# The last projection of a decoder layer, token-major: the residual is turned to tokens by VectorE and the output is stored by tokens

## The chip, the cores and the metric

The kernel runs on one core of a Trainium2 chip. The metric is the time of one execution in microseconds on the device. The kernel before was timed three times: 2201.19, 2201.46 and 2201.54 us, so its median is 2201.46 us.

## The reference, cut to what matters

The program is one decoder layer for 256 tokens of width 2048: a half SwiGLU block (hidden width 5632), a token-mixing block (sparse attention beside an mLSTM), and a second half SwiGLU block. Only the very end is touched here:

```python
def rms_norm(x, gain):
    y = x32 * lax.rsqrt(jnp.mean(x32 * x32, axis=-1, keepdims=True) + EPS)
    return y * gain

def swiglu(x, w_gate, w_up, w_down):
    return (jax.nn.silu(x @ w_gate) * (x @ w_up)) @ w_down

x = x + 0.5 * swiglu(rms_norm(x, ffn2_norm), ffn2_w_gate, ffn2_w_up, ffn2_w_down)
return x                                  # (1, 256, 2048), float32
```

The last projection is the product of the hidden values, 256 tokens by 5632, with `ffn2_w_down`, 5632 by 2048. The factor 1/rms of a token is taken out of the norm: the hidden values lack it once more, so that the last product is multiplied by 0.5 and by that token's factor before it is added to the residual.

## The kernel before, in words

**Numbers.** All weights are float32 in HBM. A weight tile (`raw`, 128 x 1024, 512 KB) comes in through the SyncE queue. ScalarE rounds it to fp32r (`whi`, an instruction that the profile calls CAST), VectorE subtracts and rounds the rest (`wlo`). Activations are kept in the same two halves, high and low. A product is the sum of three: high by high, high by low and low by high. A 128 x 1024 weight tile thus gives TensorE the same 6144 columns of moving data in every projection, cut in one of two ways.

**Token-major units** (`unit_b`, the gate and up projections). The stationary operand is a 128 x 128 piece of the activations (`XX`), the moving operand is 512 columns of the weights. The result has tokens on the partitions. A weight tile holds 2 blocks of 128 rows by 512 columns. For each block and each of the two halves of the tokens stand three matmuls of 512 columns: 12 in a tile.

**Channel-major units** (`unit_a`, the down projections and some of the mixing block). The stationary operand is a 128 x 128 piece of the weights, the moving operand is the activations of all 256 tokens. The result has channels on the partitions. A weight tile holds 4 blocks of 128 rows by 256 columns. The high and the low half of the activations lie side by side, so one matmul of 512 columns takes `whi` by both, and one of 256 columns takes `wlo` by the high half: 16 matmuls in a tile, 8 of each width. The upper and lower half of the result of the former, 256 columns each, have to be added afterwards (`fold`: a ScalarE copy and a VectorE add).

**The last projection before.** The hidden values H are channel-major (44 blocks of 128 channels, high and low). Seven channel-major units of 256 output channels and 11 weight tiles each are followed by a residual step: fold, times 0.5 and the token's factor (`RB`, the factors spread over all partitions), add to X (channel-major, in SBUF), store 128 x 2 x 256. The eighth unit (`unit_last`) has three matmuls of 256 columns for each block and each of two groups of 128 channels, 24 in a tile, and its last weight tile takes all of the first group before all of the second. So `store_last` can multiply, add and store the first group while TensorE does the second. Both groups lie in one PSUM tile. The output is 2048 channels by 256 tokens and is transposed on the host, which is no part of the time.

**What sets the order.** The program is written as one list of units; each weight tile is worked on in two halves. After each half the main loop lets at most one waiting job take a step, and issues the split of the tile that is three ahead (`whi` after the first half, `wlo` after the second). Four buffers each hold `raw`, `whi` and `wlo`. A job is a chain of pieces, each yielding between its instructions; an estimate of the engines' times decides whether one may step (`step`), and `force` runs a job to its end at once. A job may not step while both PSUM side banks (the tags "sc" or "tr") are held. Engines execute in the order in which this loop issues; each instruction waits on semaphores for its inputs and buffers.

**Turning.** `turn` moves a 128 x 512 token-major block of hidden values to channels with VectorE transposes of 32 x 32 pieces: an instruction takes 32 partitions by 256 elements, and 16 make a block of 4 x 128 channels by 256 tokens. `g_turn` is the job that does it, four instructions at a time. The last such block of the second FFN is turned during the first tiles of the down projection.

Of the kernel before, what the change touches and what calls it, by code (L numbers as in the profile page):

```python
# [9 lines left out]
F32 = mybir.dt.float32  # L10
# [4 lines left out]
OP = mybir.AluOpType  # L15
# [3 lines left out]
S = 256  # L19
D = 2048  # L20
FF = 5632
EPS = 1e-6
NEG = -1e30
KD = D // 128
KF = FF // 128
# [89 lines left out]
def layer(ctx: ExitStack, tc: tile.TileContext, xt, cols, w_small, b_in,  # L115
          wg1, wu1, wd1, w_in, cw1k, cw2k, cw1v, cw2v, wb_n, wb_m, w_out, wg2, wu2, wd2, out):
    nc = tc.nc
    est = Estimate()
    V, A, T, G = (Engine(e, n, est) for e, n in ((nc.vector, "V"), (nc.scalar, "A"), (nc.tensor, "T"), (nc.gpsimd, "G")))
# [10 lines left out]
    def nm(p):  # L130
        uid[0] += 1
        return f"{p}{uid[0]}"
# [18 lines left out]
    X = per.tile([128, KD, S], F32, name="X")  # L151
# [10 lines left out]
    RB = per.tile([128, S], F32, name="RB")  # L162
# [4 lines left out]
    def col(i, n=1):  # L167
        return cl[:, i:i + n]
# [14 lines left out]
    cur = {}  # L183
# [7 lines left out]
    def job(gen, name=None, need=(), rank=0):  # L191
        jobs.append([est.end, gen, name, need, rank])
        jobs.sort(key=lambda j: j[4])
# [55 lines left out]
    def mul(*a, **k):  # L249

        T.matmul(*a, **k)
        for _ in range(min(len(small_ones), 2 + len(small_ones) % 2)):
            small_ones.popleft()()
# [9 lines left out]
    def force(name):  # L263
        settle()
        while name not in past:
            j = next(j for j in jobs if j[2] == name)
            for n in j[3]:
                force(n)
            if step(j):
                uptake(j)  # L270
# [64 lines left out]
    def blocks(w, c0, ncol, kts):  # L335

        nk = 1024 // ncol
        v = w.rearrange("(k p) n -> p k n", p=128)
        return [(v[:, k:k + nk, c0:c0 + ncol], nk, ncol) for k in range(0, kts, nk)]
# [29 lines left out]
    def unit_last(w, c0, ncol, kts, act, done):  # L369

        nk = 1024 // ncol

        def emit(ps, h, e, wh, wl):
            a = act()
            end = h == kts // nk - 1
            for k in range(nk) if end else range(e * nk // 2, (e + 1) * nk // 2):
                kt = nk * h + k
                for c in (e,) if end else range(2):
                    cs = slice(c * 128, c * 128 + 128)
                    mul(ps[:, c, 0:S], wh[:, k, cs], a[:, kt, 0, :], start=kt == 0, stop=False)  # L380
                    mul(ps[:, c, 0:S], wh[:, k, cs], a[:, kt, 1, :], start=False, stop=False)
                    mul(ps[:, c, 0:S], wl[:, k, cs], a[:, kt, 0, :], start=False, stop=kt == kts - 1)
        u = Unit(blocks(w, c0, ncol, kts), emit, lambda ps: done(ps, 1))
        u.mid = lambda ps: done(ps, 0)
        return u
# [4 lines left out]
    def fold(o, ps, c=2):  # L390

        A.copy(o, ps[:, 0:c, S:])
        V.tensor_add(o, ps[:, 0:c, 0:S], o)

    units = []
# [23 lines left out]
    def residual(pool, c, ps, half, gcol, name):  # L419

        y = pool.tile([128, 2, S], F32, name=nm("y"), tag="y", bufs=2)
        fold(y, ps)
        if half:
            V.scalar_tensor_tensor(y, y, 0.5, rb2(), op0=OP.mult, op1=OP.mult)
        xc = X[:, 2 * c:2 * c + 2, :]
        V.tensor_add(xc, xc, y)
        if gcol is None:
            nc.sync.dma_start(ov[:, 2 * c:2 * c + 2, :], xc)
            return
        for kt in (2 * c, 2 * c + 1):  # L430
            A.activation(XH[:, kt, :], X[:, kt, :], AF.Identity, scale=col(gcol + kt))
            V.scalar_tensor_tensor(XL[:, kt, :], X[:, kt, :], col(gcol + kt), XH[:, kt, :].bitcast(F32),
                                   op0=OP.mult, op1=OP.subtract)
        if c == 0:
            A.activation(acc, xc, AF.Square)
            return
        sq = pool.tile([128, 2, S], F32, name=nm("sq"), tag="y", bufs=2)
        A.activation(sq, xc, AF.Square)
        V.tensor_add(acc, acc, sq)
        if c == 7:  # L440
            job(g_r(), name)

    ov = out.rearrange("(k p) t -> p k t", p=128)

    def store_last(pool, ps, k):
        y = pool.tile([128, S], F32, name=nm("y"), tag="y", bufs=2)
        kt = KD - 2 + k
        V.scalar_tensor_tensor(y, ps[:, k, 0:S], 0.5, RB, op0=OP.mult, op1=OP.mult)
        V.tensor_add(X[:, kt, :], X[:, kt, :], y)
        nc.sync.dma_start(ov[:, kt, :], X[:, kt, :])  # L450

    def rb2():
        return RB[:, None, :].to_broadcast([128, 2, S])

    def turn(o, h, j):

        ov_ = o.rearrange("p k (t q f) -> p t k q f", t=2, f=32)
        hv = h.rearrange("p t (k q f) -> p t k q f", q=4, f=32)
        for i in range(4):
            V.transpose(ov_[32 * j:32 * j + 32, :, :, i, :], hv[32 * i:32 * i + 32, :, :, j, :])  # L460


    def ffn(wg, wu, wd, first, nxt, name):


        env = {}

        def open_pool():
            p = tc.tile_pool(name=nm("ffn"), bufs=1)
            env["pool"] = p  # L470
            env["p"] = cur["ffn"] = p.__enter__()
            env["H"] = env["p"].tile([128, KF, 2, S], F32R, name=nm("H"), tag="h")

        def close_pool():
            env["pool"].__exit__(None, None, None)

        def gate_done(c):
            def f(ps):
                if c == 1:
                    force(first + "up")  # L480
                if c:
                    force(name + "h%d" % (c - 1))
                g = env["g", c] = env["p"].tile([128, 2, 512], F32, name=nm("sg"), tag="sg", bufs=1)
                if c:
                    gate(g, ps)
                else:
                    A.copy(g, ps)
                    job(later(gate, g, g), first + "gate", (first,))
            return f

        def gate(g, src):
            for t in range(2):
                A.activation(g[:, t, :], src[:, t, :], AF.Silu, scale=cur["R"][:, t:t + 1])

        def up_done(c):
            def f(ps):
                h = env["p"].tile([128, 2, 512], F32, name=nm("sh"), tag="sh", bufs=1)
                if c:
                    up(c, h, ps)
                else:  # L500
                    A.copy(h, ps)
                    job(later(up, c, h, h), first + "up", (first + "gate",))
            return f

        def up(c, h, src):
            V.tensor_mul(h, src, env["g", c])
            job(g_turn(c, h), name + "h%d" % c)

        def g_turn(c, h):

            ht = env["p"].tile([128, 4, S], F32, name=nm("ht"), tag="sg", bufs=1)
            H = env["H"][:, 4 * c:4 * c + 4]
            for j in range(4):
                yield
                turn(ht, h, j)
                yield
            yield
            A.copy(H[:, :, 0, :], ht)
            V.tensor_sub(H[:, :, 1, :], ht, H[:, :, 0, :].bitcast(F32))
            yield  # L520

        def later(f, *a):
            yield
            f(*a)

        def turned(u):

            emit = u.emit

            def f(ps, h, e, wh, wl):  # L530
                if h == len(u.tiles) - 2:
                    force(name + "h%d" % (FF // 512 - 1))
                emit(ps, h, e, wh, wl)
            u.emit = f
            return u

        def down_done(c):
            return lambda ps: residual(env["p"], c, ps, True, nxt, name)

        for c in range(FF // 512):  # L540
            units.append(unit_b(wg, c * 512, XH, XL, KD, gate_done(c), None if c else open_pool))
            units.append(unit_b(wu, c * 512, XH, XL, KD, up_done(c)))
        for c in range(D // 256 - (nxt is None)):
            units.append(unit_a(wd, c * 256, 256, KF, lambda: env["H"], down_done(c)))
            if c == 0:
                turned(units[-1])
        if nxt is None:
            units.append(unit_last(wd, D - 256, 256, KF, lambda: env["H"], lambda ps, k: store_last(env["p"], ps, k)))
        return close_pool


    def mixing():
# [600 lines left out]
        def out_done(c):  # L1153
            return lambda ps: residual(env["D"], c, ps, False, C_G2, "R2")
# [139 lines left out]
    for h, (u, i) in enumerate(plan):  # L1294
# [4 lines left out]
        ps = banks[u]  # L1299
        if h in range(1, KD - 4, 2):  # L1300
            x_part(h + 3, h + 5)
        wh, wl, t, _ = splits.pop(h)
        est.q["T"] = max(est.q["T"], t)
        for e in range(2):
            u.emit(ps, i, e, wh, wl)
            late = None if small_ones else cur.get("late")
            j = step()
# [13 lines left out]
    close2()  # L1321


_OUTS = [((2048, 256), 'float32')]


# [54 lines left out]
```

## Time and profile before

| | |
|---|---|
| median of three runs | 2201.46 us |
| the profiled execution: its own time, its span | 2201.03 us, 2199.3 us |
| PE, PEld, DVE, ACT busy in the span | 2187.1, 1850.3, 1430.5, 1068.7 us |
| the stretch of the last projection, first matmul to the end of the span | 1948.60 to 2199.3 us |
| its first matmul of the eighth unit; of the program's last matmul | 2163.16; 2195.47 us |
| DMA in the span | 412.41 MB, 188 GB/s |

The span lacks 1.73 us of the execution's own time, which lie around it. Matmuls overlap: the record of one is longer than the distance to the next one's start, so the rate of TensorE is read from the distances between starts. The engine names are PE for TensorE's matmuls, PEld for its loads of stationary operands, DVE for VectorE, ACT for ScalarE and SPq for the DMA queue that SyncE issues. Nearly all compute instructions carry one line number, that of a helper, so tiles are told apart by name.

### The profile page before, as it was taken

The page shows a single profiled execution, that of the slowest core. Times are in us where ns is not written, and L with a number is a line of the kernel's source. Part 1 is how long each engine was busy: PE and PEld are TensorE (multiplying, and loading weights), DVE is VectorE, ACT ScalarE, POOL GpSimd, SP SyncE. Part 2 cuts the span into 40 slices and gives each one's busy share as a digit, 9 for nine tenths or more (in the row PEclk, how much of TensorE's full clock was granted, in tenths as well). Part 3 has the DMA queues.
Part 4 walks back from the last instruction along what each step waited for, and adds up shares of the span by engine and source line. Part 5 has one row for each costly group of instructions (what it writes and reads, how often), then busy time and mean ns, then how long its engine had stood idle before and what let it go on. Part 6 is the DMA issues. An engine that isn't in the chain of part 4 may idle for free.

```text
span 2199.3 us, 29100 instructions
## 1 busy us (share of the span) xinstructions
PE 2187.1 (99%) x11241; PEld 1850.3 (84%) x11241; DVE 1430.5 (65%) x1894; ACT 1068.7 (49%) x1364; POOL 27.8 (1%) x54
## 2 busy tenths in 40 slices
PE   9999999999999999999999999999999999999999
PEld 7888888888888888777888888888888888888888
DVE  6766676665555678876777666766667666765554
ACT  6444444444444465666774455555444444443332
POOL 0000000000000000001100000000000000000000
PEclk9999999999999999999999999999999999999999
DMA  7666666666655676544556666566666666666664
GB/s 251 189 202 192 192 184 200 200 187 196 192 185 181 196 231 191 163 125 125 153 173 189 189 187 187 187 193 190 196 187 192 200 194 189 194 199 198 196 199 125
DMA packets 304987, 412.41 MB, mean 188 GB/s; under 512 B 13328, under 2 KB 195728, under 8 KB 304848
## 3 DMA queue, kind: packets, MB, share of 16 engines
q1 hardware_dynamic: 303984, 408.08, 61.2%
q0 software_dynamic: 720, 2.36, 0.4%
q8 instruction: 88, 1.44, 0.3%
q14 instruction: 51, 0.42, 0.1%
q10 hardware_dynamic: 144, 0.11, 0.0%
HBM read 408.40 MB, written 2.10 MB: 187 GB/s over the span
## 4 chain that ended last, share of the span: by engine, by line
PE 97%; DVE 1%; DMA 0%; ACT 0%; issue 0%; SPq 0%; DVEq 0%; ACTq 0%
PE mm L110 94%; PE sc L110 2%; PE tr L110 2%; DVE wlo L110 0%; DMA raw<-in_wu_dram 0%; DMA raw<-in_w_in_dram 0%; DVE nx L110 0%; DVE t L110 0%; DVE y L110 0%; ACT t L110 0%; ACT whi L110 0%; ACT kk L110 0%; DVE mo L110 0%; DVE rt L110 0%; DVE kk L110 0%
## 5 line engine op out<-in xcount | busy, mean ns | idle before, releaser
L110 DVE TENSOR_TENSOR wlo<-raw,whi 128x1024 fp32r<-128x1024 f32 (+1 forms) x771 | 934.4, 1225 | 597.0 <-ACT whi L110 591.6
L110 ACT CAST whi<-raw 128x1024 fp32r<-128x1024 f32 (+1 forms) x771 | 802.1, 1050 | 807.0 <-PE mm L110 759.0
L110 PE MATMUL mm<-whi,XX 128*128 128x512 f32 x3392 | 1060.8, 391 | 4.9 <-ACT whi L110 4.9
L110 PEld LDWEIGHTS mm<-whi,XX 128*128 128x128 f32 x3392 | 638.1, 188 | 136.2 <-ACT whi L110 4.9
L110 PE MATMUL mm<-wlo,XX 128*128 128x512 f32 x1696 | 663.1, 391 | 0.5 <-DVE wlo L110 0.5
L110 PE MATMUL mm<-H,whi 128*128 128x512 f32 (+1 forms) x1496 | 446.4, 382 | 0.5 <-DVE y L110 0.5
L110 PEld LDWEIGHTS mm<-wlo,XX 128*128 128x128 f32 x1696 | 319.2, 188 | 66.0 <-DVE wlo L110 1.8
L110 PEld LDWEIGHTS mm<-H,wlo 128*128 128x128 f32 x1408 | 264.8, 188 | 58.6
L110 PE MATMUL mm<-H,wlo 128*128 128x256 f32 x1408 | 284.2, 278 | 0.0
L110 PE MATMUL mm<-XX,whi 128*128 128x512 f32 x784 | 249.6, 399 | 0.0
L110 PEld LDWEIGHTS mm<-H,whi 128*128 128x128 f32 x1496 | 228.5, 189 | 0.9 <-DVE y L110 0.7
L110 PEld LDWEIGHTS mm<-XX,wlo 128*128 128x128 f32 x784 | 147.1, 188 | 34.8 <-DVE wlo L110 0.9
L110 DVE STREAM_TRANSPOSE ht<-sh 32x256 f32<-32x256 f32 x352 | 153.6, 436 | 6.4
L110 PE MATMUL mm<-XX,wlo 128*128 128x256 f32 x784 | 155.7, 278 | 0.2 <-DVE wlo L110 0.2
L110 PEld LDWEIGHTS mm<-XX,whi 128*128 128x128 f32 x784 | 120.6, 189 | 1.2 <-issue 0.2
L110 PE MATMUL mm<-M__10001,whi 128*128 128x512 f32 x256 | 79.9, 393 | 0.0
L110 PEld LDWEIGHTS mm<-M__10001,wlo 128*128 128x128 f32 x256 | 48.1, 188 | 10.9
L110 PE MATMUL mm<-M__10001,wlo 128*128 128x256 f32 x256 | 50.5, 278 | 0.0
L110 ACT ACTIVATE sg<-mm,R 128x512 f32<-128x512 f32 x40 | 25.4, 686 | 33.0 <-PE mm L110 31.6
L110 PE MATMUL mm<-O__5735,whi 128*128 128x512 f32 x128 | 40.3, 396 | 0.0
L110 PE MATMUL mm<-h__8408,whi 128*128 128x512 f32 x128 | 40.0, 394 | 0.0
L110 PEld LDWEIGHTS mm<-M__10001,whi 128*128 128x128 f32 x256 | 38.5, 188 | 0.0
(190 smaller groups left out, 1009.3 us busy)
## 6 DMA issues: line engine op xcount, KB each, us to landing
raw<-in_wu_dram SPq DMA_DIRECT2D x176, 512.0 KB, 4.0
raw<-in_wd_dram SPq DMA_DIRECT2D x176, 512.0 KB, 4.7
raw<-in_wg_dram SPq DMA_DIRECT2D x175, 512.0 KB, 4.5
raw<-in_w_in_dram SPq DMA_DIRECT2D x168, 512.0 KB, 4.4
raw<-in_w_out_dram SPq DMA_DIRECT2D x32, 512.0 KB, 5.0
raw<-in_wb_n_dram SPq DMA_DIRECT2D x16, 512.0 KB, 5.2
raw<-in_wb_m_dram SPq DMA_DIRECT2D x16, 512.0 KB, 4.7
bias<-in_b_in_dram POOLq DMA_DIRECT2D x9, 256.0 KB, 4.0
```

Source lines behind the costliest of these rows:

```text
L110: return g(out, *a, **k)
```

## The change

The last projection of the second FFN becomes token-major: four units of 512 output channels and 22 weight tiles, with pieces of H as the stationary operand and 512 columns of the weights as the moving one, three matmuls of 512 columns for each block and half of the tokens. A new job, `g_back`, turns the residual X back to tokens, 512 channels at a time, with 16 VectorE transposes (`turn_back`) into `xt`. After a unit, `put` takes for each half of the tokens one VectorE instruction that multiplies PSUM by 0.5 times the token's factor (`R5`, one value for each partition) and adds `xt`, and stores 128 tokens by 512 channels, 256 KB. The last unit puts the two halves of the tokens into two side banks; its last weight tile takes all of the first half before all of the second, and the first half is put between them. The output is now 256 tokens by 2048 channels.

```diff
-    def store_last(pool, ps, k):
-        y = pool.tile([128, S], F32, name=nm("y"), tag="y", bufs=2)
-        kt = KD - 2 + k
-        V.scalar_tensor_tensor(y, ps[:, k, 0:S], 0.5, RB, op0=OP.mult, op1=OP.mult)
-        V.tensor_add(X[:, kt, :], X[:, kt, :], y)
-        nc.sync.dma_start(ov[:, kt, :], X[:, kt, :])
...
+    def turn_back(o, x, i):
+        o5 = o.rearrange("p t (k q f) -> p t k q f", q=4, f=32)
+        x5 = x.rearrange("p k (t q f) -> p t k q f", t=2, f=32)
+        for j in range(4):
+            V.transpose(o5[32 * i:32 * i + 32, :, :, j, :], x5[32 * j:32 * j + 32, :, :, i, :])
...
+        def g_back(c):
+            if c == 0:
+                R5 = env["R5"] = small(2, tag="R5", bufs=1)
+                V.tensor_scalar(R5, cur["R"], 0.5, None, op0=OP.mult)
+            xt_ = env["xt", c] = env["p"].tile([128, 2, 512], F32, name=nm("xt"), tag="sg", bufs=1)
+            for i in range(4):
+                yield
+                turn_back(xt_, X[:, 4 * c:4 * c + 4, :], i)
+                yield
+
+        def unit_out(c):
+            last = c == D // 512 - 1
+            def emit(ps, h, e, wh, wl):
+                H = env["H"]
+                end = last and h == KF // 2 - 1
+                for k in range(2) if end else (e,):
+                    kt = 2 * h + k
+                    for t in (e,) if end else range(2):
+                        hh, hl = (H[:, kt, a, t * 128:t * 128 + 128] for a in range(2))
+                        mul(ps[t], hh, wh[:, k, :], start=kt == 0, stop=False)
+                        mul(ps[t], hh, wl[:, k, :], start=False, stop=False)
+                        mul(ps[t], hl, wh[:, k, :], start=False, stop=kt == KF - 1)
+            def put(ps, t):
+                if c or t == 0:
+                    force(name + "x%d" % c)
+                o = env["p"].tile([128, 512], F32, name=nm("o"), tag="o", bufs=2)
+                V.scalar_tensor_tensor(o, ps[t], env["R5"][:, t:t + 1], env["xt", c][:, t, :], op0=OP.mult, op1=OP.add)
+                nc.sync.dma_start(ov[:, t, c * 512:c * 512 + 512], o)
+            def done(ps):
+                for t in (1,) if last else range(2):
+                    put(ps, t)
+                if not last:
+                    job(g_back(c + 1), name + "x%d" % (c + 1))
+            def bank():
+                if last:
+                    return psS(), psS()
+                b = psA()
+                return b[:, 0, :], b[:, 1, :]
+            def pre():
+                job(g_back(0), name + "x0", (name + "h%d" % (FF // 512 - 1),))
+            u = Unit(blocks(wd, c * 512, 512, KF), emit, done, None if c else pre, bank)
+            if last:
+                u.mid = lambda ps: put(ps, 0)
+            return u
...
+        if nxt is None:
+            for c in range(D // 512):
+                units.append(unit_out(c))
+            turned(units[-D // 512])
+            return close_pool
-_OUTS = [((2048, 256), 'float32')]
+_OUTS = [((256, 2048), 'float32')]
```

How the order of instructions moves, at three places. All that stands ahead of the last projection keeps its order on TensorE.

TensorE, the start of the last projection. In a row, the tile that is written stands left of the arrow, the operands right of it, then the shape of the moving data. Before (a quarter of the first weight tile a pair of rows):

```order
L110 MATMUL mm_16120<-H_12656,whi_16072 128x512 x2
L110 MATMUL mm_16120<-H_12656,wlo_16073 128x256 x2
L110 MATMUL mm_16120<-H_12656,whi_16072 128x512 x2
L110 MATMUL mm_16120<-H_12656,wlo_16073 128x256 x2
L110 MATMUL mm_16120<-H_12656,whi_16072 128x512 x2
```

Now, the whole first weight tile:

```order
L110 MATMUL mm_16120<-whi_16072,H_12656 128x512
L110 MATMUL mm_16120<-wlo_16073,H_12656 128x512
L110 MATMUL mm_16120<-whi_16072,H_12656 128x512 x2
L110 MATMUL mm_16120<-wlo_16073,H_12656 128x512
L110 MATMUL mm_16120<-whi_16072,H_12656 128x512 x2
L110 MATMUL mm_16120<-wlo_16073,H_12656 128x512
L110 MATMUL mm_16120<-whi_16072,H_12656 128x512 x2
L110 MATMUL mm_16120<-wlo_16073,H_12656 128x512
L110 MATMUL mm_16120<-whi_16072,H_12656 128x512
```

Sixteen matmuls of two widths have become twelve of one width, as in the gate and up projections.

VectorE, around the end of the first of the four new units (`xt` is the residual by tokens, `o` the output, `wlo` the low half of a weight tile), now:

```order
L110 TENSOR_TENSOR wlo_16546<-raw_16489,whi_16545 128x1024
L110 SCALAR_TENSOR_TENSOR o_16555<-mm_16120,R_16265,xt_16267 128x512
L110 SCALAR_TENSOR_TENSOR o_16558<-mm_16120,R_16265,xt_16267 128x512
L110 TENSOR_TENSOR wlo_16571<-raw_16507,whi_16570 128x1024
L110 STREAM_TRANSPOSE xt_16586<-X 32x8x32 x4
L110 TENSOR_TENSOR wlo_16594<-raw_16525,whi_16593 128x1024
L110 STREAM_TRANSPOSE xt_16586<-X 32x8x32 x4
L110 TENSOR_TENSOR wlo_16616<-raw_16543,whi_16615 128x1024
L110 STREAM_TRANSPOSE xt_16586<-X 32x8x32 x4
L110 TENSOR_TENSOR wlo_16638<-raw_16568,whi_16637 128x1024
L110 STREAM_TRANSPOSE xt_16586<-X 32x8x32 x4
L110 TENSOR_TENSOR wlo_16660<-raw_16591,whi_16659 128x1024
```

The transposes for the next unit stand four at a time between the low halves of its weight tiles.

VectorE, the end of the program. Before:

```order
L110 TENSOR_TENSOR wlo_18074<-raw_17985,whi_18073 128x1024
L110 TENSOR_TENSOR wlo_18102<-raw_18015,whi_18101 128x1024
L110 SCALAR_TENSOR_TENSOR y_18177<-mm_17882,RB 128x256
L110 TENSOR_TENSOR X<-X,y_18177 128x256
L110 SCALAR_TENSOR_TENSOR y_18193<-mm_17882,RB 128x256
L110 TENSOR_TENSOR X<-X,y_18193 128x256
```

Now:

```order
L110 TENSOR_TENSOR wlo_17714<-raw_17661,whi_17713 128x1024
L110 TENSOR_TENSOR wlo_17730<-raw_17679,whi_17729 128x1024
L110 STREAM_TRANSPOSE xt_17769<-X 32x8x32 x16
L110 SCALAR_TENSOR_TENSOR o_17786<-sc_17401,R_16265,xt_17769 128x512
L110 SCALAR_TENSOR_TENSOR o_17795<-sc_17402,R_16265,xt_17769 128x512
```

The last unit holds both side banks, so the job for its residual takes no step until `put` forces it: all 16 transposes stand in one block behind the low half of the last weight tile and ahead of the two final instructions.

More of the change, by code (lines that the diff above doesn't have):

```diff
@@ L426, in residual @@
         V.tensor_add(xc, xc, y)
-        if gcol is None:
-            nc.sync.dma_start(ov[:, 2 * c:2 * c + 2, :], xc)
-            return
         for kt in (2 * c, 2 * c + 1):
@@ L441, in residual @@
             job(g_r(), name)
-    ov = out.rearrange("(k p) t -> p k t", p=128)
-    def store_last(pool, ps, k):
-        y = pool.tile([128, S], F32, name=nm("y"), tag="y", bufs=2)
-        kt = KD - 2 + k
-        V.scalar_tensor_tensor(y, ps[:, k, 0:S], 0.5, RB, op0=OP.mult, op1=OP.mult)
-        V.tensor_add(X[:, kt, :], X[:, kt, :], y)
-        nc.sync.dma_start(ov[:, kt, :], X[:, kt, :])
+    ov = out.rearrange("(t p) c -> p t c", p=128)
     def rb2():
@@ L530, in f @@
             def f(ps, h, e, wh, wl):
-                if h == len(u.tiles) - 2:
+                if h == len(u.tiles) - (2 if u.tiles[0][1] == 2 else 1):
                     force(name + "h%d" % (FF // 512 - 1))
@@ L542, in ffn @@
             units.append(unit_b(wu, c * 512, XH, XL, KD, up_done(c)))
-        for c in range(D // 256 - (nxt is None)):
+        if nxt is None:
[3 more added lines that the diff above has]
+            return close_pool
+        for c in range(D // 256):
             units.append(unit_a(wd, c * 256, 256, KF, lambda: env["H"], down_done(c)))
@@ L546, in ffn @@
                 turned(units[-1])
-        if nxt is None:
-            units.append(unit_last(wd, D - 256, 256, KF, lambda: env["H"], lambda ps, k: store_last(env["p"], ps, k)))
         return close_pool
@@ L1379 @@
     r = _run(nc, [arrays], core_ids=[0])
-    return np.ascontiguousarray(r.results[0]["out_0_dram"].T).reshape(1, 256, 2048)
+    return np.ascontiguousarray(r.results[0]["out_0_dram"]).reshape(1, 256, 2048)
```

## The prediction

> **What bounds the kernel now.** First the page: busy time by engine, and the shares of the chain of work that ended last.
>
> ```profile
> PE 2187.1 (99%) x11241; PEld 1850.3 (84%) x11241; DVE 1430.5 (65%) x1894; ACT 1068.7 (49%) x1364; POOL 27.8 (1%) x54
> PE 97%; DVE 1%; DMA 0%; ACT 0%; issue 0%; SPq 0%; DVEq 0%; ACTq 0%
> ```
>
> TensorE is the chain. A busy PE may still run below its rate, so the stretch that changes has to be read by itself. The waits from 1948.6 us on (engine, what it waited for, us, times, longest):
>
> ```profile
> ACT whi L110 <- PE mm L110: 129.4, 78, 1.8
> DVE wlo L110 <- ACT whi L110: 100.1, 65, 1.7
> PE mm L110 <- DVE y L110: 0.5, 1, 0.5
> ```
>
> ScalarE waits for TensorE, VectorE for ScalarE, and TensorE for nobody but once, 0.5 us. Weights are therefore ready ahead of it, and this stretch lasts as long as TensorE takes to issue its matmuls. What counts is the distance between their starts, not the length of their records. In the timeline of TensorE, token-major (the gate projection; start, us, count at the end):
>
> ```profile
> 1910.29 0.61 PE L110 MATMUL mm<-whi,XX 128*128 128x512 f32 x2
> 1910.74 0.39 PE L110 MATMUL mm<-wlo,XX 128*128 128x512 f32 x1
> 1910.97 0.61 PE L110 MATMUL mm<-whi,XX 128*128 128x512 f32 x2
> ...
> 1922.53 0.61 PE L110 MATMUL mm<-whi,XX 128*128 128x512 f32 x2
> ```
>
> Three matmuls of 512 columns take 0.68 us (18 such threes in 12.24 us): 226.7 ns for one, and 12 x 226.7 = 2.720 us for a weight tile. Channel-major, the down projection, by its first matmuls, and by ScalarE's copies of the first and the seventh finished unit:
>
> ```profile
> 1948.60 0.62 PE L110 MATMUL mm<-H,whi 128*128 128x512 f32 x2
> 1949.05 0.40 PE L110 MATMUL mm<-H,wlo 128*128 128x256 f32 x2
> 1949.28 0.63 PE L110 MATMUL mm<-H,whi 128*128 128x512 f32 x2
> ...
> 1979.44 0.59 ACT L110 COPY y<-mm 128x512 f32<-128x512 f32 x1 [1.97 <-PE mm L110]
> ...
> 2163.36 0.58 ACT L110 COPY y<-mm 128x512 f32<-128x512 f32 x1 [1.97 <-PE mm L110]
> ```
>
> Six units in 183.92 us are 30.65 us each, 2.787 us for a weight tile of 16 matmuls and the same 6144 columns. The eighth unit and the end of the program:
>
> ```profile
> 2163.16 0.40 PE L110 MATMUL mm<-H,whi 128*128 128x256 f32 x2
> ...
> 2183.67 0.40 PE L110 MATMUL mm<-H,whi 128*128 128x256 f32 x2
> ...
> 2184.03 0.40 PE L110 MATMUL mm<-H,whi 128*128 128x256 f32 x2
> ...
> 2193.58 0.42 DVE L110 SCALAR_TENSOR_TENSOR y<-mm,RB 128x256 f32<-128x256 f32 x1 [7.89 <-PE mm L110]
> 2194.04 0.42 DVE L110 TENSOR_TENSOR X<-X,y 128x256 f32<-128x256 f32 x1
> 2194.06 0.51 PE L110 MATMUL mm<-H,whi 128*128 128x256 f32 x2 [0.52 <-DVE y L110]
> ...
> 2194.49 2.57 SPq L450 DMA_DIRECT2D out_dram<-X  x2
> ...
> 2195.47 0.28 PE L110 MATMUL mm<-H,wlo 128*128 128x256 f32 x1
> 2195.79 0.42 DVE L110 SCALAR_TENSOR_TENSOR y<-mm,RB 128x256 f32<-128x256 f32 x1 [1.32 <-PE mm L110]
> 2196.25 0.42 DVE L110 TENSOR_TENSOR X<-X,y 128x256 f32<-128x256 f32 x1
> ```
>
> Three matmuls of 256 columns take 0.36 us, 120 ns each, and a tile of 24 takes 2.88 us. The three rates fit one rule: from 120 ns at 256 to 226.7 ns at 512 columns is 0.417 ns a column, which leaves 13.3 ns for each matmul whatever its width. More, shorter matmuls pay it more often. In the middle of the eighth unit's last tile TensorE stands still: both groups of channels lie in one PSUM tile, and VectorE's read of the first holds back the writes of the second.
>
> **TensorE's stream (the gain).** Before, from 1948.60 us to the start of the last matmul plus its 0.12 us: 2195.59 - 1948.60 = 246.99 us. The change makes 88 tiles of 12 matmuls of 512 columns, 1056 in all, in the pattern of the gate projection: 352 x 0.68 = 239.36 us. Gain 7.63 us. Split up: seven units, 7 x 30.65 against 77 x 2.720, 5.1 us; the eighth, 32.43 against 29.92 us, 2.5 us, of which 0.16 x 11 = 1.76 us is the narrow matmuls and about 0.7 us the standstill, which goes because the last unit's halves lie in two banks. The shape and not the tensor sets the rate, as a channel-major unit of the mixing block with `XX` shows:
>
> ```profile
> 1319.79 0.63 PE L110 MATMUL mm<-XX,whi 128*128 128x512 f32 x2
> ...
> 1325.37 0.63 PE L110 MATMUL mm<-XX,whi 128*128 128x512 f32 x2
> ```
>
> These are eight groups of two and two matmuls in 5.58 us, 2.79 us for a tile, with the operand that ran at 2.720 in the gate projection.
>
> The Trainium skill gives another size for the fixed part: "TensorE: Matmul & The Clock Gate", section on the back-to-back issue gap, puts the warm distance at N / 2.4 ns plus about 2.5 ns, 215.7 ns for 512 columns. Its slope agrees with the rows above; its constant does not (13.3 ns here). By the page's figures, an estimate, the stream would shrink by only 1.2 us plus the standstill.
>
> **The turn back (hidden), and the wait it could make.** 64 transposes are added; the rows of turning hidden values, and the split of a weight tile around them:
>
> ```profile
> 1946.07 1.05 ACT L110 CAST whi<-raw 128x1024 fp32r<-128x1024 f32 x1 [1.67 <-PE mm L110]
> 1947.16 1.23 DVE L110 TENSOR_TENSOR wlo<-raw,whi 128x1024 fp32r<-128x1024 f32 x1 [1.50 <-ACT whi L110]
> ...
> 1950.05 1.78 DVE L110 STREAM_TRANSPOSE ht<-sh 32x256 f32<-32x256 f32 x4
> 1951.86 1.23 DVE L110 TENSOR_TENSOR wlo<-raw,whi 128x1024 fp32r<-128x1024 f32 x1
> ...
> L110 DVE STREAM_TRANSPOSE ht<-sh x176: 426/436/443, 1516.9 to 1960.6; 32x256 f32<-32x256 f32 x176
> ```
>
> Four take 1.78 us, 0.445 each with the gaps. One out of X moves as many elements with the strides of source and target swapped; I take 0.445, below by the fastest, 0.426, above by 0.48, the mean of a VectorE instruction of 256 elements on X (first row of the next fence).
>
> Between units VectorE does two final instructions instead of three residual ones, then four times 1.78 + 1.23 us, 3.07 us with gaps against 2.72 us a tile. Its final instruction costs 0.745 us by the second row below, as it has the same form, a PSUM block times one value for each partition plus a block:
>
> ```profile
> L110 DVE SCALAR_TENSOR_TENSOR XX<-X,cl,XX 128x256 fp32r<-128x256 f32 x48 | 21.2, 482 | 13.4 <-ACT XX L110 13.4
> L110 DVE SCALAR_TENSOR_TENSOR t<-mm,R,bias 128x512 f32<-128x512 f32 x6 | 4.2, 745 | 0.4 <-PE mm L110 0.4
> ```
>
> From a unit's end U: final instructions until U+1.7, the low half of tile 3 at U+2.9, of tile 7 at U+15.2; TensorE asks for them at U+8.4 and U+19.3. Turning hidden values puts the same load on VectorE now without holding TensorE. The stores stand in SyncE's queue ahead of the next weight load, which waits until about U+2.5 behind them; landing 4.6 us later (next fence) it is there at U+7.1, and ScalarE wants it at U+8.2. So all this costs nothing; without that slack the excess counts in full at each of three places.
>
> At the end there is no such room. The last tile's `whi` starts 0.19 us after TensorE starts the tile three before (the row at 1946.07 against a tile start at 1945.88), and `wlo` ends 2.51 us after that start. With E as the stream's end, three tiles and the last make 10.88 us: VectorE is free at E-8.37, and 16 transposes of 0.445 end at E-1.2. The first half is done at E-1.36+0.20 = E-1.16, 0.20 being what lies between the stream's end and the final instruction now (2195.59 to 2195.79). They are hidden by 0.06 us; and as VectorE idles 0.62 us between the two final instructions, 0.66 us in all may be added before the end moves.
>
> **The tail (a small loss).** Before, E to the end of the span is 2199.3 - 2195.59 = 3.71 us: 0.20, two instructions to E+1.08, the store issued at E+1.11, 2.60 us for the rest. After: 0.20, one instruction of 0.745, issue at E+0.97, and a store of 256 instead of 128 KB. Issue to landing, from the DMA views of this stretch:
>
> ```profile
> raw<-in_wd_dram SPq DMA_DIRECT2D x88, 512.0 KB, 4.6
> out_dram<-X SPq DMA_DIRECT2D x7, 256.0 KB, 2.2
> out_dram<-X SPq DMA_DIRECT2D x2, 128.0 KB, 1.7
> DMA to landing us min/median/max: 1.7/2.2/3.4
> ```
>
> So 2.60 + 0.5 = 3.10 us, end at E+4.07: loss 0.36 us. Bounds: 1.7 us, as if size did not matter (loss -0.1), and 3.4 us, if it meets the first half's store, issued 1.4 us ahead (loss 1.6).
>
> Sum: 7.63 - 0.36 = 7.27 us less. The profiled execution would go from 2201.03 to 2193.76 us; it lies 0.43 us below the median of the runs, so the median goes from 2201.46 to 2194.2 us.
>
> **Rivals.** (1) The 13.3 ns do not go with the number of matmuls, and H as stationary operand runs at the channel-major rate per column: 88 x 2.787 = 245.2 us, gain 1.8 - 0.4, time 2200.1 us. For it: H was never stationary in this trace. Against it: the `XX` rows in both shapes. The page's smaller constant would end at about the same time, 2200 us. Together 7%.
>
> (2) The transpose out of X is dear, because its reads jump between channel blocks at every 32 elements. At x us each the end moves by 16(x - 0.445) - 0.66, and from x = 0.70 on the low half of tile 7 also comes late, by 16x - 11.2 us, after units one and two (1.5 us less after the first turn, which has no final instructions ahead). At twice the price, 0.89: end 6.5, places 3.0 + 3.0 + 1.5, together 14 us against 7.3 gained, 2208 us. From about 0.78 us on it is slower than before. For it: no such read is in the trace. Against it: the writes of `ht` have those strides and cost 0.436. 5%, and 3% for a price in between (0.65 to 0.85) that leaves some 2197 to 2205 us.
>
> (3) Store or VectorE at the end are late by 1 to 2 us: 2195 to 2196 us, inside the forecast's own range.
>
> **How the numbers follow.** Two tenths of a per cent, 4.4 us, is about what a measurement of this kernel tells from no change; faster means below 2197.1. Forecast with (3): 85%, all faster. Rival (1), 7%, is no change; rival (2) is slower with 5%, and its middle prices split 1% to no change and 2% to slower. So faster 0.85, same 0.08, slower 0.07. The range: below, tail and store at their lower bound and 0.5 us for the runs' spread and the rounding of the rates, 2193.0; above, the store's upper bound 1.2 us more and transposes at 0.60 us (1.8 us), 2197.2.
>
> **What would show it.** In the new profile: TensorE's threes 0.68 us apart from the first `H` matmul on, 239.4 us in all; no wait of TensorE there; transposes into `xt` of 0.42 to 0.45 us, the last block over before the first half's final instruction; that instruction about 0.74 us; 4.1 us from the stream's end to the span's. A pitch above 2.75 us a tile, a wait on `wlo` after a unit's end, or VectorE busy when the last matmul ends would prove the forecast wrong.

## The result, and the profile after

The changed kernel takes 2226.55 us (median of 4 runs, 2226.41 to 2227.18), the kernel before 2201.5 us beside it (2201.19 to 2201.65). The ratio is 1.0115, with a 95% interval of 1.0104 to 1.0127: slower by 1.15%, 25 us, where 7.3 us less were forecast.

The page of the kernel after, busy time by engine and the shares of the chain:

```profile
PE 2212.7 (99%) x10801; PEld 1829.2 (82%) x10801; DVE 1448.9 (65%) x1942; ACT 1064.2 (48%) x1357; POOL 27.8 (1%) x54
PE 98%; DVE 1%; DMA 0%; ACT 0%; issue 0%; SPq 0%; DVEq 0%; ACTq 0%
```

TensorE is still nearly all of the chain. It has 440 matmuls fewer, and yet it is busy 25.6 us longer. The timeline of TensorE and VectorE in the last projection and at the end of the program:

```profile
1981.36 0.40 PE L110 MATMUL mm<-whi,H 128*128 128x512 f32 x1
...
2212.30 7.17 DVE L110 STREAM_TRANSPOSE xt<-X 32x256 f32<-32x256 f32 x16
2219.59 0.75 DVE L110 SCALAR_TENSOR_TENSOR o<-sc,R,xt 128x512 f32<-128x512 f32 x1
2220.52 0.39 PE L110 MATMUL sc<-whi,H 128*128 128x512 f32 x1
2220.95 0.75 DVE L110 SCALAR_TENSOR_TENSOR o<-sc,R,xt 128x512 f32<-128x512 f32 x1 [0.61 <-PE sc L110]
```

The new projection is what it was forecast to be: from its first matmul at 1981.36 us to the start of the last plus 0.227 us it takes 239.39 us, against 239.36 us. From there to the end of the span (2225.0 us) it is 4.25 us, against 4.07. The stretch that was changed is 243.64 us long and was 250.70 us: 7.06 us less.

The loss lies ahead of it. The last projection now begins at 1981.36 us and began at 1948.60 us: 32.8 us later, after work of which not one instruction was altered on TensorE. The gate and up projections of the second FFN, in the timeline of TensorE:

```profile
1699.72 0.63 PE L110 MATMUL mm<-whi,XX 128*128 128x512 f32 x2
1700.19 0.40 PE L110 MATMUL mm<-wlo,XX 128*128 128x512 f32 x1
1700.43 0.63 PE L110 MATMUL mm<-whi,XX 128*128 128x512 f32 x2
...
1711.63 0.63 PE L110 MATMUL mm<-whi,XX 128*128 128x512 f32 x2
```

Three matmuls now take 0.70 us (17 threes in 11.91 us), and took 0.68 us. The same in 100 us of this stage, first before, then after (busy us and number of instructions of PE, PEld, DVE, ACT and POOL; then the granted clock, the DMA share and GB/s):

```profile
1600.00:1700.00 100.00, 100.00 (x443) 82.81 (x442) 69.66 (x90) 43.47 (x44) 0.00 (x0) 1.00 0.64 187
```

```profile
1600.00:1700.00 100.00, 100.00 (x431) 80.30 (x430) 61.63 (x73) 43.37 (x44) 0.00 (x0) 1.00 0.64 187
```

TensorE is busy without a break in both, at the full granted clock (1.00) in both, and the stretch holds 443 matmuls before and 431 after. A wait cannot be found, since there is none: each matmul occupies TensorE some 6.5 ns longer.

A table over all of the trace shows which ones. It gives the mean distance in ns from one start to the next, of consecutive matmuls less than 0.45 us apart, by operands.

| moving operand over stationary, width | count, after | before | after |
|---|---|---|---|
| weights over stationary `XX`, 512 | 5084 | 228.9 | 235.0 |
| `XX` over stationary weights, 256 | 784 | 115.7 | 118.6 |
| `XX` over stationary weights, 512 | 783 | 236.5 | 236.2 |
| H over stationary weights, first FFN, 512 | 704 | 233.1 | 233.1 |
| H over stationary weights, first FFN, 256 | 704 | 115.2 | 115.2 |
| weights over stationary H, first three units of the last projection, 512 | 792 | - | 226.7 |

In this table only matmuls with `XX` have become slower: 5084 x 6.1 ns and, where `XX` moves, 784 pairs of a 512 and a 256 x 2.6 ns make 33 us. (The means of `XX` hold a few short stalls; the medians of the first row are 227 and 234 ns.) What sets `XX` apart is its place. The change's new tile `R5`, 8 bytes in a partition, was put into the pool `per` of small tiles, where it takes 32. All that is allocated behind this pool has moved up by 32 bytes: the weight tiles, H, and most tiles of the mixing block. `XX` lies in a pool at the other end of SBUF and has not moved. In the programs' own lists of allocations, in bytes from the start of a partition:

```
              before    after
XX            196576   196576
first whi      59360    59392
H              92128    92160
```

Before, all three were equal modulo 512 (480). After, weights and H are still equal (0), and `XX` is not.

### The profile page after: what moved, and what is told of

It reads as the page before. It is cut to its first block, busy times and chain, and to the rows that moved or that the text cites. A ratio compares the mean times of both kernels' runs of the same rounds, so it can differ in the third digit from the quotient of the medians.

```text
span 2225.0 us, 28264 instructions
## 1 busy us (share of the span) xinstructions
PE 2212.7 (99%) x10801; PEld 1829.2 (82%) x10801; DVE 1448.9 (65%) x1942; ACT 1064.2 (48%) x1357; POOL 27.8 (1%) x54
## 4 chain that ended last, share of the span: by engine, by line
PE 98%; DVE 1%; DMA 0%; ACT 0%; issue 0%; SPq 0%; DVEq 0%; ACTq 0%
PE mm L110 92%; PE sc L110 4%; PE tr L110 2%; DVE wlo L110 0%; DMA raw<-in_wu_dram 0%; DMA raw<-in_w_in_dram 0%; DVE t L110 0%; DVE nx L110 0%; DVE y L110 0%; ACT kk L110 0%; ACT pt L110 0%; DVE rt L110 0%; DVE kk L110 0%; ACT whi L110 0%; ACT t L110 0%
## 5 line engine op out<-in xcount | busy, mean ns | idle before, releaser
L110 PE MATMUL mm<-H,whi 128*128 128x512 f32 x704 | 221.1, 395 | 0.0
L110 PE MATMUL mm<-whi,H 128*128 128x512 f32 x528 | 162.8, 389 | 0.0
L110 PEld LDWEIGHTS mm<-H,wlo 128*128 128x128 f32 x704 | 132.2, 188 | 31.2
L110 PE MATMUL mm<-H,wlo 128*128 128x256 f32 x704 | 138.3, 278 | 0.0
L110 PEld LDWEIGHTS mm<-whi,H 128*128 128x128 f32 x528 | 99.1, 188 | 20.6
L110 PEld LDWEIGHTS mm<-H,whi 128*128 128x128 f32 x704 | 107.2, 189 | 0.1
L110 PE MATMUL mm<-wlo,H 128*128 128x512 f32 x264 | 102.7, 389 | 0.0
L110 PE MATMUL mm<-M__10001,whi 128*128 128x512 f32 x256 | 79.9, 393 | 0.0
L110 PEld LDWEIGHTS mm<-wlo,H 128*128 128x128 f32 x264 | 49.5, 188 | 10.3
L110 PE MATMUL sc<-whi,H 128*128 128x512 f32 x176 | 54.4, 389 | 0.0
```

Of the source, the lines that this page charges most:

```text
L110: return g(out, *a, **k)
```

## The experiments

Two theories. **Place**: TensorE's rate depends on where the stationary and the moving operand lie in SBUF against each other. **New work**: something that the change does, by VectorE, the order or the stores, slows TensorE. From here on, a distance of 0 bytes means that the two operands are equal modulo 512, as in the kernel before.

**R5 in place.** The same program with `R5` in the next buffer of a tag that exists:

```diff
-                R5 = env["R5"] = small(2, tag="R5", bufs=1)
+                R5 = env["R5"] = small(2, tag="rv", bufs=2)
```

> The changed kernel with one edit: the new 8-byte tile R5 takes the next buffer of a tag that exists already, so that every tile of the kernel before is back at its old address in SBUF (R5 had moved all weight tiles and everything behind them up by 32 bytes, but not XX, which lies at the other end). Theory P (place): the 33 us were lost because the weight tiles lie 32 bytes off against XX; then threes of the gate and up projections are 0.68 us apart again, and the time is what was predicted for the change, 2194.2 us (2193.0 to 2197.2). Theory Q (the new work itself slows TensorE, through VectorE, the order or the output): nothing of the work is altered, so the time stays at 2226.5 us.

Measured: 2193.82 us (6 runs, 2193.02 to 2194.39) against 2201.13 us before; ratio 0.9967, interval 0.9954 to 0.9979. In its timeline of TensorE:

```profile
1699.97 0.61 PE L110 MATMUL mm<-whi,XX 128*128 128x512 f32 x2
1700.42 0.39 PE L110 MATMUL mm<-wlo,XX 128*128 128x512 f32 x1
1700.65 0.61 PE L110 MATMUL mm<-whi,XX 128*128 128x512 f32 x2
```

The threes are 0.68 us apart again, and the time is the forecast's 2194.2 us within 0.4. All of the new work is in this run, so the theory of new work falls.

**The kernel before, shifted.** The other half of the change by itself:

```diff
     mask4 = per.tile([128, 4], F32, name="mask4")
+    per.tile([128, 8], F32, name="gapl")
```

> The kernel before, with an unused tile of 32 bytes ahead of the weight tiles and nothing else. Theory P: all 5084 matmuls of 512 columns with XX as stationary operand take about 6.5 ns longer, 33 us in all, and the last projection (weights stationary, H moved along with them) keeps its 2.787 us a tile: 2201.5 + 33 = 2234 us. Theory Q: no new work, so 2201.5 us.

Measured: 2233.68 us, one run. Its timeline:

```profile
1700.29 0.63 PE L110 MATMUL mm<-whi,XX 128*128 128x512 f32 x2
1700.76 0.39 PE L110 MATMUL mm<-wlo,XX 128*128 128x512 f32 x1
1700.99 0.63 PE L110 MATMUL mm<-whi,XX 128*128 128x512 f32 x2
```

A tile that nothing reads or writes costs 32.5 us (one run against the median before; the nine runs before lie within 3.7 us). With the run above, the 25 us are taken apart: -7.3 for the change and +32.5 for the shift.

**Weights and XX both 32 bytes lower.** Is it an absolute place or a distance? `mask4` goes behind the weight tiles, and 32 unused bytes above `XX`; H keeps its address.

```diff
     st = ctx.enter_context(tc.tile_pool(name="stream", bufs=1))
+    per2 = ctx.enter_context(tc.tile_pool(name="per2", bufs=1))
...
     XX = xpool.tile([128, KD, 2, S], F32R, name="XX")
+    xpool.tile([128, 8], F32, name="gapr")
...
-    mask4 = per.tile([128, 4], F32, name="mask4")
+    mask4 = per2.tile([128, 4], F32, name="mask4")
```

> The changed kernel with R5 in its harmless place, weight tiles and XX both moved down by 32 bytes, H where it was. Theory P in its relative form (the distance between stationary and moving operand counts): gate and up projections stay at 0.68 us for three, the last projection (H against weights now 32 bytes off) goes to 0.70 us, 1056 x 6.5 ns = 7 us: 2194 + 7 = 2201 us. Theory P in an absolute form (a weight tile, or XX, must start at 32 bytes past a multiple of 64): gate and up at 0.70 us, 2194 + 33 = 2227 us, and the last projection slow as well if it is the weights' start.

Measured: 2201.69 us, one run. Gate projection and last projection in its timeline:

```profile
1700.23 0.62 PE L110 MATMUL mm<-whi,XX 128*128 128x512 f32 x2
1700.69 0.39 PE L110 MATMUL mm<-wlo,XX 128*128 128x512 f32 x1
1700.91 0.62 PE L110 MATMUL mm<-whi,XX 128*128 128x512 f32 x2
...
2099.61 0.63 PE L110 MATMUL mm<-whi,H 128*128 128x512 f32 x2
2100.07 0.40 PE L110 MATMUL mm<-wlo,H 128*128 128x512 f32 x1
2100.31 0.63 PE L110 MATMUL mm<-whi,H 128*128 128x512 f32 x2
```

The same weight tiles run at 0.68 us for three against `XX`, which moved with them, and at 0.70 us against H, which did not. The distance decides, not the address of either.

**Other distances.** Seven runs move the weight tiles down against `XX` and H alike, by putting small tiles that stood ahead of them behind them, in the manner of `mask4` above: the tag `R` for 64 bytes, `R` and `mask4` for 96, `mcb` for 128, `mcb` and `mask4` for 160, `mcb` and `R` for 192, `m01` for 256, `mcb` and `m01` for 384. For example:

```diff
-    mcb = per.tile([128, 2, 32], BF, name="mcb")
+    mcb = per2.tile([128, 2, 32], BF, name="mcb")
```

For 64 bytes:

> The changed kernel with R5 in its harmless place and the weight tiles moved down by 64 bytes against XX and H alike. Theory P with a period of 64 bytes: no difference, 2194 us, threes 0.68 us apart everywhere. Theory P with a longer period (128, 256 or 512 bytes; all distances were multiples of 512 before): gate, up and last projection at about 0.70 us, 2194 + 33 + 7 = 2234 us. If distance counts in steps rather than by a period, something between or below: faster than 0.68 us is possible, since the 13.3 ns that a matmul takes beyond its columns may be made of such a loss already. Theory Q: 2226.5 us.

For 96:

> The changed kernel with R5 in its harmless place and the weight tiles 96 bytes lower against XX and H. So far the token-major distance from start to start is 226.7 ns at 0 and 256 bytes, 228.9 at 192, and 233.3 at 32, 64, 128 and 384: a period of 256 bytes. If all places but the neighbourhood of 0 are equally bad, 233.3 ns and some 2231 us; 226.7 ns or less would mean a second good place. Channel-major units, where the weights are stationary, gave 345.0 ns for a matmul of 512 and one of 256 columns at 64 bytes against 348.3 at 0 bytes; is 96 lower still?

For 128:

> The changed kernel with R5 in its harmless place and the weight tiles 128 bytes lower against XX and H. What is settled: 0 bytes off gives 226.7 ns from start to start for a token-major matmul, 32 bytes about 233.3 ns, 64 bytes 233.3 ns. If the loss has a period of 128 bytes: 226.7 ns and 2194 us. If only equal places within 512 bytes are good: 233 ns, 2228 to 2234 us. If distance counts by steps, another value.

For 160:

> The same with 160 bytes. Between 128 (233.3 ns) and 192 bytes (228.9 ns): some 231 ns and 2215 us if the loss falls off steadily towards 256 bytes; a value below 226.7 ns would be a better place than the one that the kernel before has.

For 192:

> The same with 192 bytes. With a period of 128 bytes it equals 64 bytes: 233.3 ns token-major and 2228 us. With equal places alone good: the same. Steps: another value.

For 256:

> The same with 256 bytes. Period of 256 bytes or less: 226.7 ns and 2194 us. Only equal places within 512 bytes: 233 ns, 2228 to 2234 us. Steps: another value, perhaps below 226.7 ns.

For 384:

> The same with 384 bytes, which is 128 bytes off in the other direction if the period is 512. Period of 128 bytes: 226.7 ns, 2194 us. Period of 512 bytes and a loss that depends on the distance alone, not on its sign: the time of the run with 128 bytes.

Measured, one run each (2193.82 is the median of the six above, which lie within 1.4 us), with the mean distances between starts from the traces: token-major, weights over stationary H in the last projection; channel-major, H over stationary weights in the first FFN, one of 512 and one of 256 columns together. The row for 32 bytes is from the run above, where H alone was off, so its time does not compare.

| weights lower by, bytes | token-major, ns | channel-major, ns | time, us |
|---|---|---|---|
| 0 | 226.7 | 348.3 | 2193.82 |
| 32 | 233.3 | 346.7 | - |
| 64 | 233.3 | 345.1 | 2228.08 |
| 96 | 234.3 | 353.3 | 2244.61 |
| 128 | 233.3 | 348.4 | 2231.10 |
| 160 | 233.3 | 351.7 | 2239.84 |
| 192 | 228.9 | 346.7 | 2204.69 |
| 256 | 226.7 | 348.3 | 2194.52 |
| 384 | 233.3 | 348.4 | 2230.65 |

In the same 100 us of the gate and up projections, for 96, then 192, then 256 bytes:

```profile
1600.00:1700.00 100.00, 100.00 (x428) 80.51 (x427) 63.51 (x74) 42.16 (x43) 0.00 (x0) 1.00 0.66 191
```

```profile
1600.00:1700.00 100.00, 100.00 (x439) 82.04 (x438) 66.22 (x81) 43.28 (x43) 0.00 (x0) 1.00 0.64 187
```

```profile
1600.00:1700.00 100.00, 100.00 (x443) 82.84 (x442) 69.70 (x88) 43.24 (x43) 0.00 (x0) 1.00 0.65 189
```

The number of matmuls in it goes with the table: 428, 439 and 443. At the two pairs of places that lie 256 bytes apart, the values are the same: 256 is as 0, and 384 as 128, in both columns. The period of 64 that the run with 64 bytes was to try, and that of 128, fall, and so does the steady decline guessed for 160. For 96 bytes 233.3 ns and some 2231 us were expected if all places away from 0 are equally bad: it is the worst of all, in both columns. The run with 64 bytes is 6 us below its forecast of 2234 us: its channel-major units, which the forecast left alone, gained some 4 us (704 pairs x 3.3 ns with H, and by the trace about 2 us with `XX`). Token-major, 0 (or 256) is the best of the places tried, and the kernel before had it. Channel-major, where the operands have changed roles, another place is best: 64 bytes, by 3.3 ns a pair.

**A version from it.** Only the first FFN's H moves, where it is never stationary:

```diff
+            if nxt is not None:
+                env["p"].tile([128, 16], F32, name="gaph")
             env["H"] = env["p"].tile([128, KF, 2, S], F32R, name=nm("H"), tag="h")
```

> The changed kernel with R5 in its harmless place, and in the first FFN alone an unused tile of 64 bytes ahead of H, so that H as moving operand of that channel-major down projection lies 64 bytes above the stationary weights. If the distance between the two operands decides there as well, a matmul of 512 and one of 256 columns go from 348.3 to 345.0 ns: 704 pairs x 3.3 ns = 2.3 us less than the run it is compared with, 2191.5 us. If the gain with weights 64 bytes lower came from something else that moved, no difference: 2193.8 us.

Beside it on the same chip, the change with `R5` in place once more:

> The changed kernel with R5 in its harmless place once more, on the same chip as the run beside it, for the comparison of the two: 2193.8 us, 7.3 us or 0.33% below the kernel before.

Measured: 2191.50 us (5 runs, 2190.96 to 2191.98), ratio to before 0.9957, interval 0.9943 to 0.9970; and 2193.62 us (5 runs, 2193.07 to 2194.11), ratio 0.9967, interval 0.9954 to 0.9979. The down projection of the first FFN, with `R5` in place:

```profile
650.23 0.63 PE L110 MATMUL mm<-H,whi 128*128 128x512 f32 x2
...
660.68 0.63 PE L110 MATMUL mm<-H,whi 128*128 128x512 f32 x2
```

and with H 64 bytes higher:

```profile
650.09 0.62 PE L110 MATMUL mm<-H,whi 128*128 128x512 f32 x2
...
661.13 0.62 PE L110 MATMUL mm<-H,whi 128*128 128x512 f32 x2
```

Fifteen groups of two and two in 10.45 us are 0.697 us each; sixteen in 11.04 us are 0.690. Over all of the stage a pair takes 345.0 ns, as with the weights 64 bytes lower (345.1): here it does not matter which of the two operands is moved. The gain of 2.1 us was worked out ahead of the run as 2.3 us, and the two kernels' runs do not overlap. This is the fastest version here, 9.5 us below the kernel before.

## Why the prediction was wrong

**The step that failed** is the sum: "Sum: 7.63 - 0.36 = 7.27 us less." It holds what the change does to TensorE's last projection, to VectorE beside it and to the end, and no term for the 1950 us ahead of them. That all that stands ahead keeps its order on TensorE was true, and was taken to mean that it keeps its time. The missing term is +32.5 us (the shifted kernel before), over four times the rest. It comes from a line of the diff that the prediction says nothing of, the allocation of `R5`, and none of the rivals has to do with where tiles lie. The range (2193.0 to 2197.2) therefore missed, and the 7% for slower stood on another mechanism, dear transposes, that did not happen. The signs that the prediction named as proof against itself (a pitch above 2.75 us a tile, a wait after a unit's end, a late VectorE) all look at the stretch that was changed; none of them appeared there, and the kernel was slower all the same.

**TensorE's stream**: right. Forecast 239.36 us, found 239.39. Both the threes of 0.68 us and the end of the standstill are there; rival (1), the channel-major rate, is out. The sentence "the shape and not the tensor sets the rate" was too strong: with shape, widths and tensors unchanged, the distance of the operands moves a matmul of 512 columns from 226.7 to 234.3 ns. In the rows that it rested on the operands were equal modulo 512, so they could not show it. For the same reason the 13.3 ns that each matmul takes beyond its columns is the value at this distance, no constant. The trace before held a sign of it: by the rule of 13.3 ns a matmul of 512 and one of 256 columns make 346.7 ns together, and with the weights stationary they take 348.3, split as 233.1 and 115.2 in the table above where the rule says 226.7 and 120.

**The back-to-back figure.** The Trainium skill ("TensorE: Matmul & The Clock Gate", section on the back-to-back issue gap) gives N / 2.4 + 2.5 ns, as the gap of an isolated matmul, and the page has 215.7 ns as measured for 512 columns. No place tried reaches it here: the best gives 226.7 ns.

**The turn back**: right. The transposes out of X, and the answer of the trace on who waited, kernel after:

```profile
L110 DVE STREAM_TRANSPOSE xt<-X x64: 425/435/442, 1998.5 to 2219.0; 32x256 f32<-32x256 f32 x64
L110 DVE SCALAR_TENSOR_TENSOR o<-mm,R,xt x6: 741/748/751, 2041.4 to 2161.8; 128x512 f32<-128x512 f32 x6
```

```profile
ACT whi L110 <- PE mm L110: 127.4, 78, 1.8
DVE wlo L110 <- ACT whi L110: 105.3, 71, 2.7
...
DVE o L110 <- PE sc L110: 0.6, 1, 0.6
```

A median of 0.435 us where 0.445 with gaps was taken, and 0.748 us for the final instruction where 0.745 was taken: rival (2) is out. TensorE waits for nobody from 1945 us on. The block of 16 at the end ran from 2212.30 to 2219.47 us, 0.12 us ahead of the first final instruction at 2219.59 us; the forecast had 0.06 us to spare (0.09 by its own terms: 16 x 0.445 from E-8.37 end at E-1.25, not at E-1.2). VectorE then waited 0.61 us for TensorE between the two final instructions, where the forecast had 0.62.

**The tail**: right in kind, 0.18 us short. The stores, kernel after:

```profile
out_dram<-o SPq DMA_DIRECT2D x8, 256.0 KB, 2.6
DMA to landing us min/median/max: 2.3/2.6/3.8
```

The forecast took 2.2 us for a store of 256 KB, from stores that hold two pieces of 1 KB for each partition. The stores of this output, one piece of 2 KB for each partition, took 2.3 to 3.8 us, 2.6 in the median.

**The whole**: with `R5` where it moves nothing, 2193.82 and 2193.62 us against the forecast of 2194.2 us.

## What to carry to other kernels

A new tile is part of a change, even one of 8 bytes: see which other tiles it moves, and compare the addresses of what TensorE reads, as one compares the order of instructions. When a kernel slows down with TensorE busy all the time and no wait to be found, count the matmuls in equal stretches of work that was not changed, or take the distance between their starts by operand. A pad of some tens of bytes, or a tile put into an existing buffer, tells within one run whether place is the cause.

## What the runs showed of the hardware that was not expected

The time from one fp32r matmul to the next depends on the distance in SBUF between its stationary and its moving operand. With the weights as the moving operand, a matmul of 512 columns takes 226.7 ns at 0 and 256 bytes, 228.9 ns with the moving operand 192 bytes lower, and 233.3 to 234.3 ns at 32, 64, 96, 128, 160 and 384 bytes lower. At 32 bytes higher it is slow too (431 matmuls in 100 us, against 443). If the pattern repeats after 256 bytes, 192 lower is 64 higher, and the two sides of 0 are not alike: 228.9 ns at 64 higher, 233.3 at 64 lower. With the weights as the stationary operand the best distance was 64 bytes (weights lower) and the worst 96, 345.1 against 353.3 ns for a pair of matmuls.

The records of the loads of stationary operands stay at 187 to 188 ns in the median in every run. They lie beside the matmuls (PE is busy for 100.00 us of the 100 above, PEld for 82.81 of the same), so two reads of SBUF may run at once, and a conflict between them that repeats after 256 bytes would fit the table; that is argued and not shown. The Trainium skill ("TensorE: Matmul & The Clock Gate", Part 2, the first phase of a matmul) says that TensorE reads the two operands through two independent ports, so that loading the next weights takes no read bandwidth from the running matmul. In these runs the pace of the matmuls is not independent of how the two operands lie to each other. The Trainium skill ("SBUF — State Buffer", section on operand start alignment) has an operand start at a multiple of its element size, and says that this is about legality, not speed. All the places tried here are legal by it, and they differ by up to 7.6 ns a matmul.

Open stay the mechanism, whether the period of 256 bytes holds at distances other than the two pairs tried, distances that are no multiple of 32 bytes, other data types, and whether a place between those tried is better than 226.7 ns.
